# Hybrid decoder layer on one core: the last two token tiles take v's first weight chunks in turn, the convolution's sum of squares is multiplied later, and a quartet's first sum queues behind the split of its first block

## The chip, the cores and the metric

The kernel runs on one core of one Trainium2 chip. The metric is device time in microseconds (us), as the median of several runs; before the change it is 2063.5 us over three runs (2060.89 to 2068.44). Everything is fp32. To keep fp32 precision, TensorE multiplies operands that are split into a rounded high part and the remainder (fp32r hi and lo), and each logical product is three matmuls: hi·hi, hi·lo, lo·hi. Engines are named as in the profile: PE is TensorE (PEld its weight loads), ACT ScalarE, DVE VectorE, POOL GpSimd, SP the sync engine that issues nearly all DMAs.

## The reference

One decoder layer over 512 tokens, model width 2048. Only the first part is touched by the change:

```python
hn = rms_norm(x, norm_mix_pre)                 # (512, 2048)
proj = hn @ w_in                               # 2048 -> 6 x 1024
q, k, v, gate_b, gate_c, hc = split(proj)
a = rms_norm(diff_attention(q, k, v, lam, rel_bias), subln_gain) * (1 - lambda_init)
c = rms_norm(gate_b * short_conv(gate_c * hc, conv_w), conv_norm_gain)
mix = concatenate([a, c]) @ w_out
x = x + rms_norm(mix, norm_mix_post)
f = (silu(rms_norm(x) @ w_gate) * (rms_norm(x) @ w_up)) @ w_down
x = x + rms_norm(f, norm_ffn_post)
```

## The kernel before

**Stages.** The tokens are four tiles t = 0 to 3 of 128. `first_norm(t)` squares a tile on ACT (L225), scales its rows on DVE (L131), transposes it in 16 pieces on PE (L233, banks `pt_pre`), splits the result into hi and lo in `acts` (ACT L100, DVE L101), and copies the transposed tile back into the buffer of `x` (ACT L236). Half of v is multiplied plainly: `v_part(t, q4)` is 12 matmuls of 512 columns (L125 to L127) of tile t with chunk q4 of v's weights. Chunks 0 and 1 lie in the four ring tiles, chunks 2 and 3 in the spots a3, s, a4, a5. `v_out(t)` splits a finished bank `pv` (ACT, then DVE) and stores it. Order before: tiles 0 and 1 complete; then tile 2 is normed and takes its four chunks, then tile 3 is normed and takes its four.

**Quartets.** The rest of the input projection runs as 22 "quartets" q = 0 to 21: 256 columns of `w_in` as a 2 x 2 block problem, done in Strassen's way with seven products instead of eight. The products carry the numbers i = 1, 2, 5, 7, 6, 3, 4; the text writes (q, i). Each is 24 matmuls of 256 columns. `in_order` lists them: (0,1), (1,1), (0,2), (1,2), then (0,5), (0,7), (0,6), (0,3), (0,4), the same five of quartet 1, then whole quartets in the order 1, 5, 7, 2, 6, 3, 4. The names of banks are `pi_a`, `pi_b`, `pi_d`.

A product needs two operands. The weight side `w_i` is made per product by `in_prepare(n)`: a sum or difference of blocks on DVE (`in_combine`: L317 for s1, which (q,5) takes; L319, L321, L323 for the following ones, each on the one before), a hi cast on ACT (L100) and a lo subtraction on DVE (L101). It lies in one of four ring tiles, so at most four are ahead. The token side consists of sums of the halves of the transposed tiles, made once: `i1` (tiles 2, 3 less 0, 1: L249, split L254 apart into `acts`), `i3` (L254 and spots a0, a1), `i2` (L258, spots a2, a3; (q,6) takes it), `i4` (L262, spots a4, a5; (q,4) takes it). `in_gather` takes results out of the banks; L375 copies `pi_a` and so waits for a product's end.

**What sets the order.** The code is traced in the order written; a scheduler in the framework then lays each engine's instructions in one queue, by its own estimates of when they will be ready. After that every engine is strictly first in, first out.

**The convolution.** Quartets 0 to 11 are h, c, b four times. `in_finish` of each b multiplies the gate in (L421), squares on ACT (L423) and adds to `sqacc` on DVE (L429). The last one starts `conv_norm`, a side generator that advances one `yield` per product: it multiplies the four tiles of `sqacc` with a column of ones (L452, bank `p4`, in the profile `p`), takes the root on POOL, puts it on diagonals (DVE L456), multiplies with ones again (L461, bank `prc`) and scales the eight rows of y (DVE L465).

Of the kernel before, what the change touches and what calls it, by code (L numbers as in the profile page):

```python
# [21 lines left out]
NT = S // P  # L22
# [33 lines left out]
def trunk(ctx: ExitStack, tc: tile.TileContext, a, out):  # L56
# [41 lines left out]

    def split(hi, lo, src):
        nc.scalar.copy(hi, src)  # L100
        nc.vector.tensor_tensor(out=lo, in0=src, in1=hi.bitcast(F32), op=ALU.subtract)  # L101

    def rsqrt_mean(ss, n, width, eps, name):
        v = small.tile([P, n], F32, tag=f"v{n}", name=f"v_{name}")
# [115 lines left out]
    def first_norm(t):  # L220
        xn = spot(f"a{2 * (t % 2)}")
        ss = small.tile([P, 2], F32, tag="ss2", name=f"ss_{t}")
        for c in range(2):
            cs = slice(c * 1024, (c + 1) * 1024)
            nc.scalar.activation(xn[:, cs], xts[t][:, cs], AF.Square, accum_out=ss[:, c : c + 1])  # L225
        nc.vector.tensor_add(ss[:, 0:1], ss[:, 0:1], ss[:, 1:2])
        r = rsqrt_mean(ss[:, 0:1], 1, D, EPS, f"pre{t}")
        for k4 in range(4):
            scale_rows(xn, xts[t], r, gB, k4)
            b = aux_bank(f"pt_pre{t}_{k4}")  # L230
            for i in range(4):
                k = 4 * k4 + i
                nc.tensor.transpose(b[:, i * P : (i + 1) * P], xn[:, k * P : (k + 1) * P], ident)  # L233
            sl = slice(4 * k4, 4 * k4 + 4)
            split(*(x_[:, t, sl, :].rearrange("p k n -> p (k n)") for x_ in (ffn_hi, ffn_lo)), b)
            nc.scalar.copy(xts[t][:, k4 * 512 : (k4 + 1) * 512], b)  # L236
# [30 lines left out]
    def bias_rows():  # L267

        t = spot("r0")
        oh, rb, vec = t[:NB, :VL], t[:NB, VL : VL + NH], t[:NH, 1024 : 1024 + VL]  # L270
        nc.sync.dma_start(oh, a["bucket_rows"])
        nc.sync.dma_start(rb, a["rel_bias"])
        for i in range(2):
            b = aux_bank(f"pvec_{i}")
            nc.tensor.matmul(b[:NH, : VL // 2], lhsT=rb, rhs=oh[:, i * (VL // 2) : (i + 1) * (VL // 2)], start=True, stop=True)
            nc.vector.tensor_copy(vec[:, i * (VL // 2) : (i + 1) * (VL // 2)], b[:NH, : VL // 2])
        d1 = dram.tile([NH, VL], F32, name="d1")
        nc.scalar.dma_start(d1, vec)
        d2 = dram.tile([P, NH, VL], F32, name="d2")
        nc.scalar.dma_start(d2, bass.AP(d1.tensor, d1.offset, [[0, P], [VL, NH], [1, VL]]))  # L280
        return d2
# [31 lines left out]
    def in_combine(q, s):  # L313
        (p11, p21), (p12, p22) = ((r[:, :, :P], r[:, :, P:]) for r in in_raws[q])
        if s == 1:
            it["s1"] = in_slot("s1").rearrange("p (k m) -> p k m", k=8)
            nc.vector.tensor_add(it["s1"], p21, p22)  # L317
        elif s == 3:
            nc.vector.tensor_sub(p21, p11, p21)  # L319
        elif s == 2:  # L320
            nc.vector.tensor_sub(p21, p22, p21)  # L321
        else:
            nc.vector.tensor_sub(p12, p12, p21)  # L323

    def in_prepare(n):
        if n >= len(in_order):
            return
        q, i = in_order[n]
        (p11, p21), (p12, p22) = ((r[:, :, :P], r[:, :, P:]) for r in in_raws[q])
        src = {1: p11, 2: p12, 3: p12, 4: p22, 5: it.get("s1"), 6: p21, 7: p21}[i]  # L330
        if i == 7 and q >= 2:
            in_combine(q, 3)
        if i == (3 if q == in_last else 6):
            in_combine(q, 2)
        if i == 3:
            in_combine(q, 4)
        w = ring_tile(16, P, f"w_i{q}_{i}", "still").rearrange("p (a k) m -> p a k m", a=2)
        split(w[:, 0], w[:, 1], src)
        in_ops[n] = w
        if i == 4 and q + 2 <= in_last:  # L340
            load_in(q + 2)
# [103 lines left out]

    def conv_norm():

        yield
        p4 = aux_bank("p4")
        sqacc = it["sqacc"]  # L450
        for t in range(NT):
            nc.tensor.matmul(p4[:, t : t + 1], lhsT=sqacc[:, t * P : (t + 1) * P], rhs=ones[:, 0:1], start=True, stop=True)  # L452
        rc = rsqrt_mean(p4[:, :NT], NT, 1024, EPS, "conv")
        dg = in_slot("sqacc").rearrange("p (t n) -> p t n", n=P)
        for t in range(NT):
            nc.vector.tensor_scalar_mul(dg[:, t, :], ident, rc[:, t : t + 1])  # L456
        yield
        yield
        yield
        prc = aux_bank("prc")  # L460
        nc.tensor.matmul(prc, lhsT=ones, rhs=dg.rearrange("p t n -> p (t n)"), start=True, stop=True)  # L461
        for p in range(4):
            for j in range(2):
                y = it["y", p][:, j, :]
                nc.vector.scalar_tensor_tensor(  # L465
                    out=y, in0=prc, scalar=gcv[:, 2 * p + j : 2 * p + j + 1], in1=y, op0=ALU.mult, op1=ALU.mult
                )
            if p % 2:
                yield
# [10 lines left out]
    def in_proj(_):  # L480
        ready = 4
        for n, (q, i) in enumerate(in_order):
            in_product(n)
            yield
            in_gather(n)
            if n == 2:
                in_combine(0, 1)
                in_combine(0, 3)
            if q == 0 and i in (6, 3):
                in_combine(1, {6: 1, 3: 3}[i])  # L490
            elif 0 < q < in_last and i == 3:
                in_combine(q + 1, 1)
            while ready < n + (3 if n < 4 else 4):
                in_prepare(ready)
                ready += 1
            if n == 3:
                i2(0)
                i2(1)
            if n == 4:
                i4(0)  # L500
                i4(1)
            if i == 5 and q > 0:
                in_finish(q - 1)
            if n == 8:
                small_inputs()
            if q == in_last and i == 2:
                conv_split(0)
            if q == in_last and i == 3:
                conv_split(1)
                preloaded["o0_2"] = load_chunk(*out_spec(0, 2))  # L510
        in_finish(in_last)
# [49 lines left out]
        lambda n: [spot(f"a{ {3: 0, 2: 2, 4: 4}[n] + i}", F32R) for i in range(2)],  # L561
    )

    for t in range(2, NT):
        first_norm(t)
        if t == 2:
            d2 = bias_rows()
            load_in(0)
        else:
            i1(0, (0,))  # L570
            i1(1, (0,))
            i3(0)
            i3(1)
            v_out(0)
            v_out(1)
            v_out(2)
            load_in(1)
        for q4 in range(4):
            v_part(t, q4)
            if t == NT - 1 and q4 < 2:  # L580
                in_prepare(2 * q4)
                in_prepare(2 * q4 + 1)
            if t == NT - 1 and q4 == 1:
                i1(0, (1,))
                i1(1, (1,))
    v_out(3)
    add_job([], in_proj, ahead=0)

# [760 lines left out]
```

## Time and profile before

| what | value |
|---|---|
| median of three runs | 2063.5 us (2060.89 to 2068.44) |
| the profiled execution | 2065.88 us, of which 2063.8 us from first to last instruction |
| mean granted TensorE clock in it | 0.993 |
| ACT busy, DVE busy | 49%, 83% |
| DMA | 346.11 MB, mean 168 GB/s |

In a timeline row stand the start in us, the busy us, engine, line, operation, out<-in, shape and count, and in brackets how long the engine sat idle before it and what ended that. A row of the waits view gives the engine and line that waited, for whom, and then total us, times, longest us. A row of windows gives each engine's busy us in a stretch, then the granted clock (PEclk, 1.00 is full speed), the DMA share and GB/s.

### The profile page before, as it was taken

How to read it: one execution, taken by the hardware profiler on the slowest of the kernel's cores; microseconds unless marked ns; L12 is line 12 of the kernel's file. 1: busy time of each engine (PE TensorE's matmuls, PEld its weight loads, DVE VectorE, ACT ScalarE, POOL GpSimd, SP SyncE). 2: the span in 40 equal slices, each digit the busy share in tenths (PEclk: the TensorE clock that was granted, in tenths of full speed). 3: DMA queues.
4: the chain of work that ended last, by engine and by line, in shares of the span. 5: the costliest groups of instructions: out<-in, count | busy, mean ns of one | idle time of the engine just before them, and what ended most of it. 6: DMA issues, size and time to landing. Idle time of an engine off the chain costs nothing.

```text
span 2063.8 us, 37998 instructions
## 1 busy us (share of the span) xinstructions
PE 2010.3 (97%) x16158; PEld 1941.6 (94%) x16158; DVE 1713.5 (83%) x2141; ACT 1008.1 (49%) x1421; POOL 24.9 (1%) x44
## 2 busy tenths in 40 slices
PE   7999999999999998999999999999999999999998
PEld 5899999999788887999999999999999999999996
DVE  6898889887676689989889989989888687878886
ACT  5555454445576464454455545545545344334442
POOL 0000000000000000000000000000000000000000
PEclk9999999999999999999999999999999999999999
DMA  7533333444663643654554545546546937648354
GB/s 247 156 123 99 107 123 121 166 165 145 207 212 102 233 167 108 186 159 139 174 158 150 170 151 166 175 130 189 164 126 194 346 111 255 210 124 304 108 185 154
DMA packets 310026, 346.11 MB, mean 168 GB/s; under 512 B 12985, under 2 KB 271033, under 8 KB 307425
## 3 DMA queue, kind: packets, MB, share of 16 engines
q1 hardware_dynamic: 308544, 338.95, 50.7%
q10 hardware_dynamic: 1312, 4.74, 0.7%
q8 instruction: 126, 2.06, 0.4%
q14 instruction: 44, 0.35, 0.1%
HBM read 283.87 MB, written 62.41 MB: 168 GB/s over the span
## 4 chain that ended last, share of the span: by engine, by line
PE 74%; DVE 13%; DMA 6%; issue 3%; ACT 2%; SPq 1%; POOL 0%; DVEq 0%; POOLq 0%; ACTq 0%
PE pb L127 6%; PE pb L125 6%; PE pb L126 6%; PE pd L126 6%; PE pd L127 6%; PE pd L125 6%; PE pa L125 5%; PE pa L126 5%; PE pa L127 5%; PE pi_b L127 2%; PE pi_b L126 2%; PE pi_b L125 2%; DVE w L101 2%; DVE w_i L101 2%; PE pi_a L127 2%
## 5 line engine op out<-in xcount | busy, mean ns | idle before, releaser
L100 ACT CAST w<-raw_q 128x1024 fp32r<-128x1024 f32 x130 | 136.7, 1052 | 163.3 <-PE pb L127 72.5
L127 PE MATMUL pb<-acts,w 128*128 128x256 f32 x704 | 195.7, 278 | 3.7 <-DVE w L101 3.7
L125 PE MATMUL pb<-acts,w 128*128 128x256 f32 x704 | 195.4, 278 | 1.6 <-ACT w L100 1.6
L127 PE MATMUL pa<-acts,w 128*128 128x256 f32 x704 | 195.0, 277 | 1.9 <-DVE w L101 1.8
L126 PE MATMUL pb<-acts,w 128*128 128x256 f32 x704 | 195.3, 277 | 0.0
L125 PE MATMUL pa<-acts,w 128*128 128x256 f32 x704 | 194.9, 277 | 0.3 <-ACT w L100 0.3
L127 PE MATMUL pb<-x,w 128*128 128x256 f32 x704 | 194.8, 277 | 0.3 <-DVE w L101 0.2
L125 PE MATMUL pb<-x,w 128*128 128x256 f32 x704 | 194.6, 276 | 0.0
L126 PE MATMUL pb<-x,w 128*128 128x256 f32 x704 | 194.6, 276 | 0.0
L126 PE MATMUL pa<-acts,w 128*128 128x256 f32 x704 | 194.5, 276 | 0.0
L126 PE MATMUL pd<-w_d,acts 128*128 128x256 f32 x640 | 179.1, 280 | 3.4 <-DVE w_d L101 3.4
L125 PE MATMUL pd<-w_d,acts 128*128 128x256 f32 x640 | 178.6, 279 | 1.3 <-DMA acts<-hx 1.3
L127 PE MATMUL pd<-w_d,acts 128*128 128x256 f32 x640 | 178.5, 279 | 0.6 <-DMA acts<-hx 0.6
L101 DVE TENSOR_TENSOR w<-raw_q,w 128x1024 fp32r<-128x1024 f32 x130 | 158.1, 1217 | 4.1 <-ACT w L100 4.0
L127 PEld LDWEIGHTS pb<-acts,w 128*128 128x128 f32 x704 | 133.3, 189 | 4.1 <-DVE w L101 4.1
L125 PEld LDWEIGHTS pb<-acts,w 128*128 128x128 f32 x704 | 133.2, 189 | 1.8 <-ACT w L100 1.8
L127 PEld LDWEIGHTS pa<-acts,w 128*128 128x128 f32 x704 | 132.1, 188 | 2.5 <-DVE w L101 2.5
L126 PE MATMUL pd<-w_d,x 128*128 128x256 f32 x480 | 133.5, 278 | 0.0
L125 PE MATMUL pd<-w_d,x 128*128 128x256 f32 x480 | 133.3, 278 | 0.0
L127 PE MATMUL pd<-w_d,x 128*128 128x256 f32 x480 | 133.2, 278 | 0.0
L126 PEld LDWEIGHTS pb<-acts,w 128*128 128x128 f32 x704 | 133.2, 189 | 0.0
L127 PEld LDWEIGHTS pb<-x,w 128*128 128x128 f32 x704 | 132.4, 188 | 0.6 <-DVE w L101 0.6
(322 smaller groups left out, 6895.5 us busy)
## 6 DMA issues: line engine op xcount, KB each, us to landing
raw_q<-in_w_gate SPq DMA_DIRECT2D x44, 1024.0 KB, 5.5
r_i<-in_w_in SPq DMA_DIRECT2D x22, 1024.0 KB, 5.4
raw_i<-in_w_in SPq DMA_DIRECT2D x22, 1024.0 KB, 5.2
post<-in_w_up SPq DMA_DIRECT2D x22, 1024.0 KB, 5.2
pre<-in_w_up SPq DMA_DIRECT2D x22, 1024.0 KB, 5.9
hx<-spare SPq DMA_DIRECT2D x20, 896.0 KB, 8.4
hx<-m SPq DMA_DIRECT2D x20, 896.0 KB, 9.5
raw_o<-in_w_out SPq DMA_DIRECT2D x16, 1024.0 KB, 5.4
```

Of the source, the lines that this page charges most:

```text
L100: nc.scalar.copy(hi, src)
L101: nc.vector.tensor_tensor(out=lo, in0=src, in1=hi.bitcast(F32), op=ALU.subtract)
L125: nc.tensor.matmul(o, lhsT=lhi, rhs=rhi, start=start, stop=False, **kw)
L126: nc.tensor.matmul(o, lhsT=lhi, rhs=rlo, start=False, stop=False, **kw)
L127: nc.tensor.matmul(o, lhsT=llo, rhs=rhi, start=False, stop=stop, **kw)
```

## The change

Four edits in the first 360 us; the arithmetic is the same.

- **v in turn.** Tile 3 is normed right after the first chunk of tile 2, and its `i1` and `i3` follow. Tiles 2 and 3 then take chunk 0/1, 2 and 3 in turn. `i2`, and the sums s1 and the next difference of quartet 0, are traced before the last chunks, `i4` within the first products; `v_out(2)` comes after tile 2's last chunk. From the third product on (before: the fifth) one operand more is kept ahead.
- **The sum of squares later.** `conv_norm` waits six products instead of one before `p4`, and six instead of three before `prc`.
- **First sums behind a split.** `split` returns its DVE instruction, and s1 of the next quartet (L317) is put behind the last split that was traced, that of (q+1, 1), in DVE's queue. Before, the scheduler was free to put it earlier.

```diff
     def split(hi, lo, src):
         nc.scalar.copy(hi, src)
-        nc.vector.tensor_tensor(out=lo, in0=src, in1=hi.bitcast(F32), op=ALU.subtract)
+        return nc.vector.tensor_tensor(out=lo, in0=src, in1=hi.bitcast(F32), op=ALU.subtract).ins
...
-        split(w[:, 0], w[:, 1], src)
+        it["split"] = split(w[:, 0], w[:, 1], src)
...
     def conv_norm():
-        yield
+        for _ in range(6):
+            yield
         p4 = aux_bank("p4")
...
-        yield
-        yield
-        yield
+        for _ in range(6):
+            yield
         prc = aux_bank("prc")
...
-            if n == 2:
-                in_combine(0, 1)
-                in_combine(0, 3)
             if q == 0 and i in (6, 3):
                 in_combine(1, {6: 1, 3: 3}[i])
             elif 0 < q < in_last and i == 3:
-                in_combine(q + 1, 1)
-            while ready < n + (3 if n < 4 else 4):
+                with tc.issue_after(it["split"]):
+                    in_combine(q + 1, 1)
+            while ready < n + (3 if n < 2 else 4):
                 in_prepare(ready)
                 ready += 1
-            if n == 3:
-                i2(0)
-                i2(1)
-            if n == 4:
-                i4(0)
-                i4(1)
+            if n in (1, 2):
+                i4(n - 1)
...
-    for t in range(2, NT):
-        first_norm(t)
-        if t == 2:
-            d2 = bias_rows()
-            load_in(0)
-        else:
-            i1(0, (0,))
-            i1(1, (0,))
-            i3(0)
-            i3(1)
-            v_out(0)
-            v_out(1)
-            v_out(2)
-            load_in(1)
-        for q4 in range(4):
-            v_part(t, q4)
-            if t == NT - 1 and q4 < 2:
-                in_prepare(2 * q4)
-                in_prepare(2 * q4 + 1)
-            if t == NT - 1 and q4 == 1:
-                i1(0, (1,))
-                i1(1, (1,))
+    first_norm(2)
+    d2 = bias_rows()
+    load_in(0)
+    v_part(2, 0)
+    first_norm(3)
+    for tau in range(2):
+        i1(tau, (0,))
+        i3(tau)
+    v_out(0)
+    v_out(1)
+    load_in(1)
+    v_part(2, 1)
+    for q4 in range(2):
+        v_part(3, q4)
+        in_prepare(2 * q4)
+        in_prepare(2 * q4 + 1)
+    for tau in range(2):
+        i1(tau, (1,))
+    for t in (2, 3):
+        v_part(t, 2)
+    i2(0)
+    i2(1)
+    in_combine(0, 1)
+    in_combine(0, 3)
+    v_part(2, 3)
+    v_out(2)
+    v_part(3, 3)
     v_out(3)
```

What the queues hold now, at three places. First ACT, from the end of v into the first products. In the names, `w_i0_6` is the weight operand of (0,6), `a2` to `a5` are the token sums of `i2` and `i4`, `pi_a0` and `pi_a1` the banks of quartets 0 and 1. Before:

```order
L100 CAST x3_i23_255<-pv_3_107 128x512
L100 CAST w_i0_5_665<-s_i31_662 128x1024
L100 CAST a2_i32_696<-x0_i14_108 128x1024
L100 CAST w_i0_7_692<-raw_i0_0_393 128x1024
L375 COPY s_i31_662<-pi_a0_588 128x256
L375 COPY s_i31_662<-pi_a1_613 128x256
L100 CAST a2_i32_696<-x1_i16_182 128x1024
L100 CAST w_i0_6_730<-raw_i0_0_393 128x1024
```

and after the change:

```order
L100 CAST x2_i22_253<-pv_2_106 128x512
L100 CAST x3_i23_255<-pv_3_107 128x512
L100 CAST a2_i31_553<-x0_i14_108 128x1024
L100 CAST a2_i31_553<-x1_i16_182 128x1024
L100 CAST w_i0_5_678<-s_i33_560 128x1024
L375 COPY s_i33_560<-pi_a0_599 128x256
L100 CAST w_i0_7_681<-raw_i0_0_393 128x1024
L375 COPY s_i33_560<-pi_a1_624 128x256
L100 CAST a4_i34_650<-x0_i14_108 128x1024
L100 CAST w_i0_4_771<-raw_i0_1_394 128x1024
L100 CAST a4_i34_650<-x1_i16_182 128x1024
L100 CAST w_i0_6_712<-raw_i0_0_393 128x1024
```

The token sums of `i4` (a4) and the operand of (0,4) have moved ahead of the operand of (0,6), and the casts of the last two v banks now stand in a row.

DVE holds the partners of these casts. Between the copies above and the operand of (0,6) stood before

```order
L101 TENSOR_TENSOR w_i0_7_692<-raw_i0_0_393,w_i0_7_692 128x1024
L258 TENSOR_TENSOR x1_i16_182<-x3_i23_255,x1_i16_182 128x1024
L321 TENSOR_TENSOR raw_i0_0_393<-raw_i0_1_394,raw_i0_0_393 128x8x128
L262 TENSOR_TENSOR x0_i14_108<-x0_i14_108 128x1024
L101 TENSOR_TENSOR a3_i33_697<-x1_i16_182,a2_i32_696 128x1024
L101 TENSOR_TENSOR w_i0_6_730<-raw_i0_0_393,w_i0_6_730 128x1024
```

and now

```order
L101 TENSOR_TENSOR w_i0_7_681<-raw_i0_0_393,w_i0_7_681 128x1024
L101 TENSOR_TENSOR a5_i35_651<-x0_i14_108,a4_i34_650 128x1024
L262 TENSOR_TENSOR x1_i16_182<-x1_i16_182 128x1024
L321 TENSOR_TENSOR raw_i0_0_393<-raw_i0_1_394,raw_i0_0_393 128x8x128
L101 TENSOR_TENSOR w_i0_4_771<-raw_i0_1_394,w_i0_4_771 128x1024
L101 TENSOR_TENSOR a5_i35_651<-x1_i16_182,a4_i34_650 128x1024
L101 TENSOR_TENSOR w_i0_6_712<-raw_i0_0_393,w_i0_6_712 128x1024
```

so `i4` is finished before the split for (0,6), where before it was finished behind it. Behind these rows DVE goes on with L323, L380, L387, L317 (s1 of quartet 1), the split of (0,3), L383 and the split of (1,5).

Third, PE. Where (0,6) gives over to (0,3), PE had before the 24 matmuls of (0,3) without a break, and (1,5) after (0,4). Now one matmul of (1,5), bank `pi_b1`, stands within (0,3):

```order
L127 MATMUL pi_d0_778<-a2_i31_553,w_i0_6_712 128x256
L125 MATMUL pi_b0_715<-acts_72,w_i0_3_742 128x256
L126 MATMUL pi_b0_715<-acts_72,w_i0_3_742 128x256
L125 MATMUL pi_b1_882<-acts_72,w_i1_5_807 128x256
L127 MATMUL pi_b0_715<-acts_72,w_i0_3_742 128x256
```

And the sum of squares stood between (12,2) and (12,6),

```order
L126 MATMUL pi_a12_3137<-acts_72,w_i12_2_3163 128x256
L127 MATMUL pi_a12_3137<-acts_72,w_i12_2_3163 128x256
L452 MATMUL p4_3253<-ones_78,x3_i23_255 128x1 x4
L125 MATMUL pi_a12_3137<-a2_i32_696,w_i12_6_3192 128x256
L126 MATMUL pi_a12_3137<-a3_i33_697,w_i12_6_3192 128x256
```

and stands now between (13,5) and (13,7), five products on:

```order
L126 MATMUL pi_b13_3376<-acts_72,w_i13_5_3315 128x256
L127 MATMUL pi_b13_3376<-acts_72,w_i13_5_3315 128x256
L453 MATMUL p4_3401<-ones_78,x3_i23_255 128x1 x4
L125 MATMUL pi_b13_3376<-a0_i27_456,w_i13_7_3344 128x256
L126 MATMUL pi_b13_3376<-a1_i28_457,w_i13_7_3344 128x256
```

On DVE the two L429 that finish `sqacc` stand where they stood, behind the split of (12,6); `prc` comes between (14,1) and (14,5), where it was ahead of (13,1), and the eight L465 stand between L323 of quartet 14 and the split of (14,6).

## The prediction

> **What bounds the kernel now.** First the page, for who is busy; then PE's own waits; then the windows and PE's timeline where those waits lie.
>
> ```profile
> PE 2010.3 (97%) x16158; PEld 1941.6 (94%) x16158; DVE 1713.5 (83%) x2141; ACT 1008.1 (49%) x1421; POOL 24.9 (1%) x44
> ```
>
> PE works nearly without a break, so an edit that removes no matmul can only win PE's gaps. The waits of PE over the whole span, longest first:
>
> ```profile
> PE pt_pre L233 <- DVE a_i L131: 9.6, 1, 9.6
> ...
> PE p L452 <- issue: 2.9, 1, 2.9
> PE pi_b L127 <- DVE w_i L101: 2.8, 3, 1.5
> ...
> PE pi_d L127 <- DVE w_i L101: 1.2, 1, 1.2
> ...
> PE pi_b L125 <- ACT w_i L100: 0.3, 1, 0.3
> ```
>
> The 9.6 us at the start are out of the change's reach. The other four rows, 7.2 us, all lie in the input projection, which it reorders. The windows place them and show the clock:
>
> ```profile
> 45.00:50.00 5.00, 5.00 (x27) 3.04 (x26) 3.02 (x6) 3.12 (x6) 0.00 (x0) 1.00 0.04 0
> ...
> 90.00:95.00 5.00, 3.47 (x30) 3.28 (x29) 5.00 (x7) 2.10 (x2) 0.00 (x0) 1.00 0.71 217
> 95.00:100.00 5.00, 4.63 (x38) 4.22 (x36) 5.00 (x9) 1.34 (x2) 0.10 (x1) 1.00 0.41 119
> 100.00:105.00 5.00, 4.21 (x36) 4.21 (x37) 4.57 (x8) 3.11 (x5) 0.00 (x0) 1.00 0.32 113
> 105.00:110.00 5.00, 3.76 (x33) 3.56 (x32) 5.00 (x7) 3.22 (x4) 0.00 (x0) 1.00 0.16 44
> 320.00:325.00 5.00, 3.04 (x14) 3.08 (x15) 3.49 (x6) 1.91 (x3) 0.93 (x1) 0.61 0.74 229
> 325.00:330.00 5.00, 5.00 (x34) 5.00 (x33) 3.10 (x8) 1.32 (x2) 0.09 (x1) 0.71 0.57 194
> ```
>
> From 90 to 110 DVE is full and PE is not: DVE is late with the first quartets' operands. From 320 to 330 there is a second loss beside the wait: the granted clock falls to 0.61 and 0.71.
>
> **The first quartets.** PE's timeline, with the first matmul of (0,5), of (0,3), the four stops, and the first of (1,3):
>
> ```profile
> 83.45 0.28 PE L125 MATMUL pi_b<-acts,w_i 128*128 128x256 f32 x1
> ...
> 91.61 0.28 PE L125 MATMUL pi_b<-acts,w_i 128*128 128x256 f32 x1
> ...
> 93.52 0.39 PE L127 MATMUL pi_b<-acts,w_i 128*128 128x256 f32 x1 [1.53 <-DVE w_i L101]
> ...
> 99.40 0.39 PE L125 MATMUL pi_b<-acts,w_i 128*128 128x256 f32 x1 [0.28 <-ACT w_i L100]
> ...
> 100.79 0.39 PE L127 MATMUL pi_b<-acts,w_i 128*128 128x256 f32 x1 [0.88 <-DVE w_i L101]
> ...
> 107.86 0.39 PE L127 MATMUL pi_d<-a_i,w_i 128*128 128x256 f32 x1 [1.24 <-DVE w_i L101]
> ...
> 110.55 0.28 PE L125 MATMUL pi_b<-acts,w_i 128*128 128x256 f32 x1
> ```
>
> Three products without a wait take 91.61 - 83.45 = 8.16 us: 2.72 us each, 0.113 us a matmul. From (0,5) to (1,3) are eight products, 21.8 us; they took 27.1. So 5.3 us are lost here, 3.9 in waits and the rest in restarts. That is the most this part can win. Why DVE was idle before, and at what pace it works after:
>
> ```profile
> 59.53 1.91 PE L233 MATMUL pt_pre<-ident,a_i 128*128 128x128 f32 x16
> ```
>
> ```profile
> 60.78 1.89 DVE L101 TENSOR_TENSOR acts<-pt_pre,acts 128x512 fp32r<-128x512 f32 x3 [6.25 <-ACT acts L100]
> ...
> 92.25 1.22 DVE L101 TENSOR_TENSOR w_i<-raw_i,w_i 128x1024 fp32r<-128x1024 f32 x1
> 93.39 0.41 DVE L380 TENSOR_TENSOR x_i<-x_i 128x256 f32<-128x256 f32 x1
> 93.73 1.22 DVE L101 TENSOR_TENSOR a_i<-x_i,a_i 128x1024 fp32r<-128x1024 f32 x1
> ```
>
> DVE waited 6.25 us for tile 3's transposes, behind all of tile 2's v. The change puts them after one chunk, three chunks (36 matmuls, about 8 us) earlier, so DVE can start the token sums sooner. PE's work up to (0,5) is the same in number, and I find no new wait there: (0,5) still starts at 83.45. But ACT's queue has changed too:
>
> ```profile
> 83.65 0.37 ACT L375 COPY s_i<-pi_a 128x256 f32<-128x256 f32 x1 [2.34 <-PE pi_a L127]
> 84.42 1.06 ACT L100 CAST a_i<-x_i 128x1024 fp32r<-128x1024 f32 x1 [0.40 <-DVE x_i L258]
> ```
>
> The second L375 waits for the fourth product, in either order. Before, the casts of (0,5) and (0,7) were ahead of it; now the cast of `i4` and all that follows stand behind it, and DVE stands behind ACT. I follow the new queues by these durations (a 1024-wide DVE step takes 1.14 us before the next, a 256-wide one 0.34):
>
> - ACT: L375 to 84.0, cast of `i4` to 85.1. DVE from 85.1: five 1024-wide steps, then the split of (0,6) from 90.8 to 92.0. Its hi cast, behind L321, is done at 89.6.
> - PE: (0,6) is due at 88.9, its third matmul, the first with lo, at 89.1. It stops twice, about 0.7 and 2.2 us, and goes on at 92.0.
> - PE ends (0,6) at 94.5, does two matmuls of (0,3) and comes at 94.7 to the stray one of (1,5). For that DVE does L323, L380, L387, L317 from 91.9 to 95.0 and ACT casts to 96.1: 1.4 us of waiting.
> - From there no operand is late. The closest is (1,6), split done by 105.7, due at 106.9. (1,3) starts at 109.4, and with 0.1 us for each of three restarts at 109.7.
>
> So this part gives 110.55 - 109.7 = 0.8 us, not 5.3: the idle time of DVE before 60 is won, but given back to waits behind ACT. Its ends are -1 (each of the two chains a step of 1.14 us later) and 5.3 (no wait).
>
> On SP the loads of quartet 2 now stand behind all stores of v and four small loads. They need the buffer that the split of (0,6) frees at 92.0 in any case, and their operands are due behind (1,4), after 109; I cost this at nothing, cover some 10 us. Holding one operand more from the third product on uses ring tiles that are free by then, and is in the order above.
>
> **The sum of squares.** The rows around it:
>
> ```profile
> 312.67 0.28 PE L126 MATMUL pi_b<-a_i,w_i 128*128 128x256 f32 x1
> 313.30 0.38 PE L127 MATMUL pi_b<-a_i,w_i 128*128 128x256 f32 x1 [0.35 <-DVE w_i L101]
> ...
> 318.74 0.28 PE L127 MATMUL pi_a<-acts,w_i 128*128 128x256 f32 x1
> 321.95 1.84 PE L452 MATMUL p<-ones,x_i 128*128 128x1 f32 x8 [2.94 <-issue]
> 323.66 0.56 PE L125 MATMUL pi_a<-a_i,w_i 128*128 128x256 f32 x1
> ...
> 328.13 0.28 PE L125 MATMUL pi_a<-a_i,w_i 128*128 128x256 f32 x1
> ...
> 333.93 1.02 PE L461 MATMUL prc<-x_i,ones 128*128 128x512 f32 x2
> ```
>
> ```profile
> 309.62 1.23 DVE L317 TENSOR_TENSOR s_i<-r_i,r_i 128x1024 f32<-128x1024 f32 x1 [3.50 <-DMA r_i<-in_w_in]
> ...
> 312.02 1.22 DVE L101 TENSOR_TENSOR w_i<-raw_i,w_i 128x1024 fp32r<-128x1024 f32 x1
> ...
> 321.17 0.68 DVE L429 TENSOR_TENSOR x_i<-x_i,x_i 128x512 f32<-128x512 f32 x1
> ...
> 336.29 5.35 DVE L465 SCALAR_TENSOR_TENSOR x_i<-prc,gcv,x_i 128x512 f32<-128x512 f32 x8
> ```
>
> "issue" hides DVE: the last L429 ends at 321.85, PE starts at 321.95. After it come the narrow matmuls and 21 normal ones at 0.21 us each. From 318.85 to 328.13 are 9.3 us. Unhindered, the 21 take 2.4, and the eight narrow passes 1.0 if each takes what a transpose does (1.91/16 = 0.12 us at 59.53). So 5.9 us go away if `p4` finds its sum ready. Five products later is 13.6 us, about 332; the sum has 10 us in hand. On DVE, L105 reads `p4` and now stands behind the split of (13,6); the next split behind it is that of (13,3), and PE has three products, 8.2 us, between `p4` and that. So a DVE that waits there holds nobody. If the narrow ones cost their 1.84 us still, it is 5.0.
>
> **First sums behind a split.** At 309.62 L317 of the next quartet held DVE 3.5 us for a transfer; the split behind it came late, and PE lost 313.30 - 312.67 - 0.11 = 0.5 us. With L317 behind the split, that goes. What L317 now waits for, it would have waited for anyway; behind it stand its own quartet's operands, due two products (5.4 us) later.
>
> **The sum.** 0.8 + 5.9 + 0.5 = 7.2 us: 2065.88 - 7.2 = 2058.7 for an execution like the profiled one. That lies 2.4 us above the median of the runs, and its largest loss hangs on when one transfer landed, so in a median run I take some of the 5.9 as absent already: between 2063.5 - 7.2 = 2056.3 and 2058.7, I forecast **2057.5 us**. Half a per cent is 10.3 us, about what a measurement of this kernel can tell from no change.
>
> **The rivals.**
>
> *All waits of the first quartets go* (0.15). For it: DVE's 6.25 idle us exceed the 5.3 lost. Against it: the queue of ACT above. Gain 5.3 + 5.9 + 0.5 = 11.7, so 2065.88 - 11.7 = 2054.2, and down to 2063.5 - 11.7 = 2051.8 as a median.
>
> *The eight scalings meet (14,6)* (0.14). L465 takes 5.35 us on DVE, now right ahead of the split of (14,6), which PE wants three products (8.2 us) and two matmuls after `prc`. Before, L465 began 1.3 us after `prc` ended (336.29 against 334.95); then 1.3 + 5.3 + 1.2 = 7.8 us, a reserve of 0.6. A DVE two steps (2.3 us) later makes PE wait 1.7, and a clock drop like that at 323.66 (21 matmuls at +0.1) adds 2.1: 3.8 us, 2061.3.
>
> *The clock falls at (0,6) and stays low while waits follow* (0.04); this one ends slower. At 321.95 a wait of 2.94 us and the narrow matmuls halved the clock; (0,6) would have 2.9 us. If half speed lasts from there to the end of (1,6), 142 matmuls cost 0.1 us more each, 14.2, less the 1.4 of the next wait that it swallows: 2058.7 + 12.8 = 2071.5. It decides if low clock lasts over 7 us or so. Against it: four stops up to 1.53 us left PEclk at 1.00 from 90 to 110, and matmuls split this one in two. [...] At 321.95 the trace shows the drop after 2.94 us with narrow work behind.
>
> *The clock falls at the transposes* (0.05). Tile 3's 16 transposes now come 12 matmuls after tile 2's and the bias rows:
>
> ```profile
> 45.58 1.47 PE L233 MATMUL pt_pre<-ident,a_i 128*128 128x128 f32 x12
> 46.98 0.70 PE L275 MATMUL pvec<-r_i 32*8 32x320 f32 x2
> ```
>
> If such work counted as idle, about 5 of 7.5 us from 45.6 on would, and a drop would cost as at 323.66, 2.1 us: 2060.8. Against it, 45 to 50 holds over 2 us of it (the two rows) at PEclk 1.00. [...]
>
> That `p4` waits still, in its new place, would need DVE 10 us late (0.02).
>
> **How the numbers follow.** Forecast 0.60, the named rivals 0.40. The range 2051.5 to 2063.5 reaches from the first rival's median to no gain at all. Faster by over 0.5% means under 2053.2: the lower part of the first rival and little else, 0.14. Slower by over 0.5% needs over 2073.8, above even the slow rival: 0.02.
>
> **What would show it.** Right: PE's wait at L453 gone and PEclk 1.00 from 310 to 340; L317 no longer ahead of its split; PE stops at (0,6) for 2 to 3 us and at a `pi_b` L125 for about 1.4; (1,3) starts near 109.7. Wrong: (1,3) before 107 or after 111.7; a wait of PE after 345 behind L465; PEclk under 0.9 anywhere between 45 and 340.

## The result, and the profile after

The changed kernel takes 2054.93 us in the median of six runs (2053.49 to 2057.99); the kernel before, run beside it, 2064.64 us (2059.61 to 2068.44). The ratio is 0.9961, with a 95% interval of 0.9949 to 0.9973: by the ratio some 8 us faster (the two medians lie 9.7 us apart), inside the range that was given and within half a per cent. The profiled execution took 2057.99 us, 7.9 us less than that of before, where the sum was 7.2.

So the total came out. The experiments below show that it came out for a partly wrong reason: of the three edits (the change is announced as four, but it lists three) one does it all, and it is the one that was priced at 0.5 us. First the views in which that can be read. The waits of PE in the projection, after; of the four rows of before, two are left, with other names:

```profile
PE pi_d L127 <- DVE w_i L101: 1.8, 1, 1.8
...
PE pi_d L125 <- ACT w_i L100: 0.6, 1, 0.6
```

The wait at the sum of squares and all waits of `pi_b` are gone. PE's timeline around the two that stay, from the first matmul of (0,5) to that of (1,3):

```profile
83.75 0.28 PE L125 MATMUL pi_b<-acts,w_i 128*128 128x256 f32 x1
...
89.93 0.39 PE L125 MATMUL pi_d<-a_i,w_i 128*128 128x256 f32 x1 [0.58 <-ACT w_i L100]
...
92.26 0.39 PE L127 MATMUL pi_d<-a_i,w_i 128*128 128x256 f32 x1 [1.82 <-DVE w_i L101]
...
93.18 0.41 PE L125 MATMUL pi_d<-a_i,w_i 128*128 128x256 f32 x1
...
96.38 0.38 PE L125 MATMUL pi_b<-acts,w_i 128*128 128x256 f32 x1
...
96.72 0.28 PE L125 MATMUL pi_b<-acts,w_i 128*128 128x256 f32 x1
...
110.19 0.28 PE L125 MATMUL pi_b<-acts,w_i 128*128 128x256 f32 x1
```

The two stops at (0,6) are the forecast ones (0.58 and 1.82 us, where 0.7 and 2.2 were expected). The third, at the stray matmul of (1,5) at 96.72, did not happen. Instead the matmuls from 93.18 on take 0.41 us in place of 0.28. The windows of that place, cut where the clock changes, show why:

```profile
89.77:93.18 3.41, 1.42 (x9) 1.22 (x10) 3.41 (x4) 0.59 (x2) 0.00 (x0) 1.00 0.13 32
93.18:96.59 3.41, 3.41 (x19) 3.41 (x17) 3.10 (x5) 2.10 (x2) 0.00 (x0) 0.50 0.54 178
96.59:100.00 3.41, 3.41 (x31) 3.41 (x31) 3.32 (x8) 0.25 (x1) 0.10 (x1) 1.00 1.06 353
```

For 3.41 us the granted clock is exactly half, behind a window of 3.41 us in which PE was busy for only 1.42. PE came to the stray matmul at 96.72, 2.0 us later than forecast, and by then its operand was there: the cast, forecast to end at 96.1, ended at 96.28. One loss took the place of the other.

Around the sum of squares, its narrow matmuls, and two windows where the clock had been 0.61 and 0.71:

```profile
330.51 0.95 PE L453 MATMUL p<-ones,x_i 128*128 128x1 f32 x8
```

```profile
320.00:325.00 5.00, 5.00 (x47) 5.00 (x46) 4.82 (x7) 2.37 (x3) 0.00 (x0) 1.00 0.34 122
325.00:330.00 5.00, 5.00 (x47) 5.00 (x46) 4.93 (x5) 3.43 (x4) 0.00 (x0) 1.00 0.25 100
```

No stop, full clock, and 0.95 us for the eight narrow passes, which took 1.84 at half clock before. And DVE, which feeds them:

```profile
312.18 1.41 DVE L429 TENSOR_TENSOR x_i<-x_i,x_i 128x512 f32<-128x512 f32 x2
...
319.38 1.22 DVE L317 TENSOR_TENSOR s_i<-r_i,r_i 128x1024 f32<-128x1024 f32 x1
...
350.47 5.35 DVE L465 SCALAR_TENSOR_TENSOR x_i<-prc,gcv,x_i 128x512 f32<-128x512 f32 x8
355.74 1.21 DVE L101 TENSOR_TENSOR w_i<-raw_i,w_i 128x1024 fp32r<-128x1024 f32 x1
```

Here is the row that should give pause. The last L429 ends at 313.6, 8.3 us earlier than before (321.85). But that sum was not moved, only the matmuls that read it. PE starts (12,6), ahead of which `p4` used to stand, at 316.91: `p4` would have found its sum ready in its old place too.

### The profile page after: what moved, and what is told of

It reads as the page before. It is cut to its first block, busy times and chain, and to the rows that moved or that the text cites. A ratio compares the mean times of both kernels' runs of the same rounds, so it can differ in the third digit from the quotient of the medians.

```text
span 2056.2 us, 37995 instructions
## 1 busy us (share of the span) xinstructions
PE 2009.8 (98%) x16158; PEld 1942.2 (94%) x16158; DVE 1714.6 (83%) x2141; ACT 1010.1 (49%) x1421; POOL 26.2 (1%) x44
## 4 chain that ended last, share of the span: by engine, by line
PE 83%; DVE 8%; DMA 3%; issue 2%; ACT 2%; SPq 1%; POOL 0%; DVEq 0%; POOLq 0%; ACTq 0%
PE pb L127 6%; PE pb L126 6%; PE pb L125 6%; PE pd L126 6%; PE pd L127 6%; PE pd L125 6%; PE pa L127 5%; PE pa L126 5%; PE pa L125 5%; PE pi_b L125 4%; PE pi_b L127 4%; PE pi_b L126 4%; PE pi_a L125 3%; PE pi_a L127 3%; PE pi_a L126 3%
## 5 line engine op out<-in xcount | busy, mean ns | idle before, releaser
L127 PEld LDWEIGHTS pb<-acts,w 128*128 128x128 f32 x704 | 132.9, 189 | 3.2 <-DVE w L101 3.2
L127 PEld LDWEIGHTS pa<-acts,w 128*128 128x128 f32 x704 | 132.8, 189 | 2.2 <-DVE w L101 2.2
L125 PEld LDWEIGHTS pb<-acts,w 128*128 128x128 f32 x704 | 132.9, 189 | 1.8 <-ACT w L100 1.8
L125 PEld LDWEIGHTS pa<-acts,w 128*128 128x128 f32 x704 | 132.9, 189 | 0.4 <-ACT w L100 0.4
```

The costliest lines, as they stand in the source:

```text
L125: nc.tensor.matmul(o, lhsT=lhi, rhs=rhi, start=start, stop=False, **kw)
L127: nc.tensor.matmul(o, lhsT=llo, rhs=rhi, start=False, stop=stop, **kw)
```

## The experiments

Three stretches of the projection are compared, read off the starts of products in PE's timeline: A from (0,5) to (1,3), eight products; B from (12,2) to (14,6), fifteen products, with `p4` and `prc` in it; C from (14,6) to (15,1), three products behind the eight scalings.

| kernel | A | B | C | ratio to before (95%) |
|---|---|---|---|---|
| before | 27.10 | 49.15 | 8.17 | 1 |
| changed | 26.44 | 43.20 | 8.17 | 0.9961 (0.9949 to 0.9973) |
| e1: v in turn alone | 26.74 | 49.58 | 8.16 | 0.9999 (0.9988 to 1.0009) |
| e2: sum later alone | 26.96 | 44.22 | 12.35 | 0.9997 (0.9988 to 1.0006) |
| e3: split order alone | 26.28 | 43.09 | 8.16 | 0.9962 (0.9949 to 0.9976) |
| e4: v in turn + split order | 26.32 | 43.10 | 8.16 | 0.9963 (0.9950 to 0.9977) |
| e5: sum later + split order | 26.49 | 43.20 | 8.16 | 0.9965 (0.9952 to 0.9978) |
| e6: changed + four orders | 22.21 | 43.20 | 8.16 | 0.9951 (0.9938 to 0.9963) |
| e8: e3 + four orders | 26.75 | 43.10 | 8.16 | 0.9975 (0.9963 to 0.9987) |
| e10: changed, again | 26.32 | 43.21 | 8.16 | 0.9971 (0.9962 to 0.9981) |
| e11: e6, again | 22.27 | 43.21 | 8.16 | 0.9959 (0.9943 to 0.9975) |

### One edit at a time

e1 is the changed kernel with the other two edits undone:

```diff
     def conv_norm():
-        for _ in range(6):
-            yield
+        yield
         p4 = aux_bank("p4")
...
-        for _ in range(6):
-            yield
+        yield
+        yield
+        yield
         prc = aux_bank("prc")
...
-                with tc.issue_after(it["split"]):
-                    in_combine(q + 1, 1)
+                in_combine(q + 1, 1)
```

> Only v in turn (with i2, i4 and the deeper look-ahead); the sum of squares and the first sums as before. Theory (the parts add up, each in its own place): (0,5) to (1,3) shrinks from 27.1 us to about 26.4 as in the changed kernel, one stop of 0.6 and 1.8 us at (0,6) in place of four; p4 still stops PE for about 2.9 us and half clock follows; L317 still takes 3 us or so waiting for a transfer. 0.4 to 0.8 us faster than before, so about 2064. Rival (a DVE that starts earlier stays ahead): the stop at p4 shrinks below 1.5 us and the clock there stays at 1.00; 5 us faster, about 2059.5.

2061.18 us against 2061.57: no change. A is 0.36 us shorter, B 0.43 us longer. DVE's wait for the transfer ("the hold" from here on) is 3.68 us where it was 3.50, and PE's stop 2.93 us where it was 2.94:

```profile
308.38 1.23 DVE L317 TENSOR_TENSOR s_i<-r_i,r_i 128x1024 f32<-128x1024 f32 x1 [3.68 <-DMA r_i<-in_w_in]
...
319.93 0.68 DVE L429 TENSOR_TENSOR x_i<-x_i,x_i 128x512 f32<-128x512 f32 x1
```

```profile
320.71 1.83 PE L452 MATMUL p<-ones,x_i 128*128 128x1 f32 x8 [2.93 <-issue]
```

The theory holds for where the time is lost (its gain of 0.4 to 0.8 us is too small to be seen in the ratio), and the rival falls: DVE's early start in v does not reach as far as the sum of squares, since L317 waits for a transfer in quartet after quartet, 17 times and 37.5 us in all.

e2 is the kernel before with the six and six `yield`s alone.

> Only the sum of squares later (6 and 6 products). Theory: the stop at p4 and the half clock behind it go, 5.9 us; but with L317 free to stand ahead of its split, DVE comes late behind the eight scalings: (14,6) waits 0.5 to 1.9 us, and perhaps (14,3) and (15,1) too. Gain 4 to 5.4 us, about 2059.5. Rival (the edit needs no help): no wait after 345, gain 5.9, about 2058.7. The first quartets keep their four stops and 27.1 us in both.

2061.28 us against 2061.57: no change either. B shrinks by 4.9 us, as wanted, but C grows by 4.2. DVE and PE behind the new place of the scalings:

```profile
347.85 1.23 DVE L317 TENSOR_TENSOR s_i<-r_i,r_i 128x1024 f32<-128x1024 f32 x1 [2.17 <-DMA r_i<-in_w_in]
...
355.39 5.35 DVE L465 SCALAR_TENSOR_TENSOR x_i<-prc,gcv,x_i 128x512 f32<-128x512 f32 x8
360.66 1.21 DVE L101 TENSOR_TENSOR w_i<-raw_i,w_i 128x1024 fp32r<-128x1024 f32 x1
```

```profile
361.93 0.39 PE L127 MATMUL pi_a<-a_i,w_i 128*128 128x256 f32 x1 [2.16 <-DVE w_i L101]
```

```profile
359.38:362.79 3.41, 1.25 (x11) 1.05 (x10) 3.41 (x6) 1.04 (x1) 0.00 (x0) 1.00 0.00 0
362.80:366.21 3.41, 3.41 (x18) 3.41 (x18) 3.41 (x4) 1.05 (x1) 0.00 (x0) 0.50 0.46 134
```

This is the prediction's rival of the eight scalings, come true in a kernel that lacks the third edit: L317 waits 2.17 us for its transfer, everything behind it is late, (14,6) stops for 2.16 us, and half clock follows. It was priced at 3.8 us; it costs 4.2. My expectation for this run had the waits but not the clock: 4 to 5.4 us of gain, where the projection's last product starts 1.5 us earlier than before (504.58, 506.10) and the time shows none; its interval would still allow 2.5 us. In the changed kernel the same split ends at 355.74 + 1.21 = 356.95, and (14,6) starts at 357.39.

e3 is the kernel before with only this:

```diff
-        nc.vector.tensor_tensor(out=lo, in0=src, in1=hi.bitcast(F32), op=ALU.subtract)
+        return nc.vector.tensor_tensor(out=lo, in0=src, in1=hi.bitcast(F32), op=ALU.subtract).ins
...
-        split(w[:, 0], w[:, 1], src)
+        it["split"] = split(w[:, 0], w[:, 1], src)
...
             elif 0 < q < in_last and i == 3:
-                in_combine(q + 1, 1)
+                with tc.issue_after(it["split"]):
+                    in_combine(q + 1, 1)
```

> Only L317 behind the split of its quartet's first block. Theory: the wait of 0.35 us at (12,7) goes and two delays of 0.2 and 0.45 us around 131 and 260 with it; the stop at p4 and the low clock stay, the first quartets too. 0.5 to 1.3 us faster, about 2063.5. Rival (a later s1 makes the products 5 late): stops at pi_b L125 between 110 and 500, 1 us or more in sum, and no gain.

2053.97 us against 2061.57, the whole gain of the change. Both my theory (0.5 to 1.3 us) and its rival (no gain) were wrong. The stop at `p4` is gone with `p4` in its old place:

```profile
311.23 1.41 DVE L429 TENSOR_TENSOR x_i<-x_i,x_i 128x512 f32<-128x512 f32 x2
...
320.16 1.22 DVE L317 TENSOR_TENSOR s_i<-r_i,r_i 128x1024 f32<-128x1024 f32 x1
```

```profile
315.96 0.95 PE L452 MATMUL p<-ones,x_i 128*128 128x1 f32 x8
```

The two L429 run in a row and end at 312.6, 3.3 us ahead of `p4`. How much this one wait held DVE in the kernel before stands in the waits of DVE:

```profile
DVE s_i L317 <- DMA r_i<-in_w_in: 16.1, 9, 3.5
...
DVE s_i L317 <- DMA raw_i<-in_w_in: 11.0, 8, 3.5
```

Seventeen holds, 27.1 us in all. In the changed kernel and in e3 DVE has no such row: 10 us later in the queue, the transfer has landed. Most of the holds cost PE little, because DVE had time to catch up before an operand was due: from (1,3) to (12,2) PE is 1.36 us faster in e3 than before. The hold at 309.62 was followed by the two L429 and by a PE that waits for them.

The order moves more than the hold. Before, L317 and L319 of the next quartet stood ahead of the sum (2.4 us, from 309.62 to 312.02), and a split stood between the two L429 (1.1 us, at 320.04); in e3 these are behind the sum too. So 3.5 us of waiting and 3.5 us of work left the place ahead of `p4`. Either of them is about as long as what PE lost there, 2.94 us at `p4` and 0.64 at (12,7). That this row's place made the sum late is shown; how much of it was the wait and how much the work, no run separates.

### The edits in pairs

e4 is the changed kernel with the old `yield`s, e5 is e3 with the new ones.

> The changed kernel with the sum of squares put back to one and three products. Theory now (the stop at p4 came from L317 waiting ahead of its split, so the sum's new place wins nothing once L317 is behind): no stop at p4 in its old place, PEclk 1.00 from 310 to 340, and the projection as long as in the changed kernel within 0.3 us; about 8 us under before, ratio 0.996. Rival, as forecast (the place of p4 decides): the stop of about 2.9 us and the half clock are back, 6 us more than the changed kernel.

> The sum of squares later and L317 behind its split, v in the old order. Theory now: the same as the split alone, (0,5) to (1,3) 26.3 us with its three or four stops, no stop after 112, no wait behind the eight scalings; ratio 0.996. Rival: the scalings at their new place still make (14,6) late without the deeper look-ahead, 0.5 us or more after 345.

2053.74 and 2053.72 us against 2062.2. The theory formed after e3 holds in both: B is 43.1 to 43.2 us wherever `p4` stands, and C is 8.16. With L317 behind its split, the sum's new place wins nothing, and v in turn wins nothing that the time or the stretch A shows (26.3 to 26.5 us in e3, e4, e5 and the changed kernel).

### What v in turn could have won

ACT's rows in the changed kernel show what holds it there:

```profile
83.95 0.37 ACT L375 COPY s_i<-pi_a 128x256 f32<-128x256 f32 x1 [1.40 <-PE pi_a L127]
84.22 1.05 ACT L100 CAST a_i<-x_i 128x1024 fp32r<-128x1024 f32 x1
86.67 1.05 ACT L100 CAST w_i<-raw_i 128x1024 fp32r<-128x1024 f32 x1 [1.40 <-PE pi_b L127]
...
88.83 1.05 ACT L100 CAST w_i<-raw_i 128x1024 fp32r<-128x1024 f32 x1
```

L375 at 83.95 was named in the prediction. But there is a second wait of the same kind: the cast at 86.67 is that of (0,4). It writes the ring tile that (0,5) must first give back, and it stands ahead of the cast of (0,6) at 88.83. e9 mends the first alone, in a single execution:

```diff
...
+        it["cast"] = late["cast"]
...
-            nc.scalar.copy(it["q1", q], pq["a"][:, :256])
+            with tc.issue_after(it["cast"]):
+                nc.scalar.copy(it["q1", q], pq["a"][:, :256])
```

> The changed kernel with one more order: L375 behind the last cast traced. This is the row that the prediction named as what holds ACT. Prediction's theory (L375 is what makes (0,6) late): the stops at (0,6) shrink from 2.4 to under 0.5 us. Rival (the cast of (0,4), which waits for a ring tile ahead of the cast of (0,6), is the second half): the two stops shrink only to about 0.5 and 1.3 us, and only together with the casts in order, as in e6_queue_order, do they go.

A is 25.63 us; its one time, 2050.7 us, gives no verdict. The stops of PE in A:

```profile
88.85 0.39 PE L125 MATMUL pi_d<-a_i,w_i 128*128 128x256 f32 x1 [0.32 <-ACT w_i L100]
...
90.48 0.38 PE L127 MATMUL pi_d<-a_i,w_i 128*128 128x256 f32 x1 [1.13 <-DVE w_i L101]
...
94.55 0.39 PE L125 MATMUL pi_b<-acts,w_i 128*128 128x256 f32 x1 [1.06 <-ACT w_i L100]
```

The prediction's single cause falls: with L375 out of the way, stops of 0.32 and 1.13 us stay at (0,6). The clock stays whole behind them: the matmuls there take 0.28 to 0.29 us, where those from 93.18 on took 0.41 in the changed kernel. And the forecast third stop, at the stray matmul of (1,5), appears with 1.06 us.

e6 puts the casts in order too, and PE and quartet 1's sums with them:

```diff
...
-        it["split"] = split(w[:, 0], w[:, 1], src)
+        with ExitStack() as order:
+            if "cast" in it and n < 12:
+                order.enter_context(tc.issue_after(it["cast"]))
+            it["split"] = split(w[:, 0], w[:, 1], src)
+            it["cast"] = late["cast"]
+            it["split", i] = it["split"]
...
+            if "pe" in it and n < 12:
+                order.enter_context(tc.issue_after(it["pe"]))
...
-                in_combine(1, {6: 1, 3: 3}[i])
+                with tc.issue_after(it["split", {6: 3, 3: 4}[i]]):
+                    in_combine(1, {6: 1, 3: 3}[i])
```

> The changed kernel with four more orders, for the first twelve products only: on ACT each operand's cast behind the cast of the product before (so (0,4) no longer goes ahead of (0,6)) and L375 behind the last cast traced; on PE each product behind the one before; on DVE quartet 1's sums behind the splits of (0,3) and (0,4). Theory (the gain of the earlier v was given back in the order of the queues): following the queues, the stops at (0,6) shrink from 2.4 to about 0.3, one of 0.4 us stands at (1,6), no drop of the clock; (0,5) to (1,3) takes 22.6 us in place of 26.4, so (1,3) starts near 106.5; 3.8 us under the changed kernel, ratio to before 0.9943. Rival (DVE has no time left there, whatever the order): (1,3) after 109, gain under 1 us.

A is 22.21 us, where eight products without any stop need 21.8. PE's waits have no row of the projection left. (0,6) begins without a gap, and (1,3) begins 4.7 us earlier than in the changed kernel:

```profile
83.25 0.28 PE L125 MATMUL pi_b<-acts,w_i 128*128 128x256 f32 x1
...
88.69 0.28 PE L125 MATMUL pi_d<-a_i,w_i 128*128 128x256 f32 x1
...
105.46 0.28 PE L125 MATMUL pi_b<-acts,w_i 128*128 128x256 f32 x1
```

e6 adds three orders to that of e9 at once, so that the cast of (0,4) is the second cause is argued from its row at 86.67 and not shown by itself.

The median is 2052.07 us. To set this beside the changed kernel, both ran again on one chip.

> The changed kernel once more, beside the next one on the same chip. The projection takes the same time as in its first profile within 0.3 us, except where the windows of the clock fall otherwise: at (0,6) with the half clock (1,3) near 110.2, and if the two stops there lie in two windows, no half clock but a stop of about 1.3 us at the stray matmul of (1,5). Ratio 0.996.

> The kernel of e6_queue_order once more. Projection 4 to 5 us shorter than in the run beside it; median 2 to 5 us below it, ratio to before 0.993 to 0.995. Rival: what it wins in the projection is lost again behind it (median the same within 1 us).

2054.85 us (12 runs) and 2052.17 us (6 runs). The stretches repeat to 0.15 us, and the gain at the end is 2.7 us of the 4 in stretch A. e11's ratio is 0.9959, short of the 0.993 to 0.995 expected, and the intervals of the two ratios overlap. That e6 beats the changed kernel is seen in the trace, in both pairs of medians and in the runs (of the twelve in e10 one, 2053.62 us, lies below the slowest of e11, 2053.71), but the ratios do not settle it.

e8 gives the same orders to e3, with v in the old order.

> The four orders of e6_queue_order and L317 behind its split, but v in the old order (tile 3 behind all of tile 2) and the sum of squares in its old place. Theory (the orders only spend the time that v in turn gives DVE): DVE still begins the token sums late, the stops at (0,3), (1,5) and (1,6) stay, (0,5) to (1,3) takes 26 to 27 us, ratio 0.996 as with the split alone. Rival (the orders alone do it): 22 to 23 us there, ratio 0.994.

A is 26.75 us: the theory holds. Its ratio, 0.9975, is above the 0.996 expected; the interval overlaps that of e3. Added to the third edit one at a time, neither v in turn nor the orders win anything in A (26.3 us with the third edit alone); together they win 4.

### The clock

e7 takes e6 and makes 14 stops:

```diff
...
+    stops = {14 + 7 * (q - 2): 1 + q % 3 for q in range(3, 21) if q not in (11, 12, 13, 14)}
+
+    def in_stop(n):
+        q1 = it["q1", in_order[n][0]][:, :P]
+        for _ in range(stops[n]):
+            nc.gpsimd.tensor_tensor(out=q1, in0=q1, in1=ones, op=ALU.mult)
+        b = aux_bank(f"stop{n}")
+        it["pe"] = nc.tensor.matmul(b[:, 0:1], lhsT=q1, rhs=ones[:, 0:1], start=True, stop=True).ins
...
+            if n in stops:
+                in_stop(n)
```

> The kernel of e6_queue_order with 14 made stops of PE: after the first product of 14 quartets, PE waits for one, two or three GpSimd passes over L375's result (a product with ones, which changes nothing), then does a narrow matmul. Theory (the clock is set by fixed windows of 3.41 us, and a window in which PE is busy under about half halves the next one): every half-clock stretch is 3.41 us long and begins at a whole multiple of 3.4133 us from the others; stops under 1.6 us never lead to one, those of 2 to 3 us only where most of the stop lies in one window, so some do and some of the same length do not. Rival (a stop's own length decides): all stops above one length are followed by half clock, all below are not, and the stretches begin at a fixed time behind the stop.

For eleven of them the windows of 3.41 us were measured: nine were followed by half clock, two were not (2.58 us of PE in the window at 133.68, 2.35 in that at 468.19). The windows with the stop, and those behind it, for three stops of the first kind and one of the second:

```profile
154.16:157.57 3.41, 1.16 (x9) 0.79 (x7) 2.56 (x3) 1.44 (x3) 2.36 (x2) 1.00 0.00 0
157.57:160.98 3.41, 3.41 (x18) 3.41 (x18) 0.00 (x0) 0.00 (x0) 0.00 (x0) 0.50 0.86 281
178.05:181.46 3.41, 0.95 (x6) 0.75 (x6) 3.41 (x3) 2.55 (x4) 2.73 (x3) 1.00 0.00 0
181.46:184.87 3.41, 2.60 (x12) 2.60 (x13) 3.29 (x5) 0.00 (x0) 0.76 (x1) 0.50 0.48 155
184.87:188.28 3.41, 3.41 (x18) 3.41 (x18) 0.00 (x0) 0.01 (x1) 0.00 (x0) 0.50 0.44 152
...
396.51:399.92 3.41, 1.69 (x12) 1.29 (x12) 3.38 (x4) 2.26 (x3) 1.22 (x1) 1.00 0.39 155
399.92:403.33 3.41, 3.41 (x18) 3.41 (x17) 1.62 (x2) 0.00 (x0) 0.00 (x0) 0.50 0.54 193
...
468.19:471.60 3.41, 2.35 (x18) 1.94 (x18) 3.13 (x3) 1.32 (x2) 0.97 (x1) 1.00 0.00 0
471.60:475.01 3.41, 3.41 (x32) 3.41 (x31) 0.27 (x1) 0.84 (x1) 0.00 (x0) 1.00 0.55 169
```

The half clock begins at 157.57 and at 399.92, 242.35 us apart, 71 times 3.4133; the stretches behind all nine of these stops, from 157.57 to 519.38, lie on that grid. Of the eleven windows, all at full clock, those with 1.69 us of PE or less were followed by half clock, those with 2.35 and 2.58 us were not.

Two points of the expectation failed. Not every stretch of half clock is 3.41 us long: the one at 181.46 takes two windows, and the first of the two, itself at half clock, held only 2.60 us of PE. Before, the half clock at `p4` did the same (2.56 us of PE at 321.11). And stops under 1.6 us did lead to half clock: PE's idle time in the window at 396.51, 1.72 us, is one of 0.92 and one of 0.80 us.

What e7 did not give is two stops of one length with different ends. That part is shown by a stop that stands in every kernel here, 1.8 us at the first matmuls of a block of the down projection. In the kernel before and in e6:

```profile
1651.48 0.39 PE L126 MATMUL pd<-w_d,acts 128*128 128x256 f32 x1 [1.80 <-DVE w_d L101]
```

```profile
1648.89:1652.30 3.41, 1.61 (x14) 1.41 (x14) 2.69 (x4) 0.00 (x0) 0.00 (x0) 1.00 1.02 320
1652.30:1655.71 3.41, 3.41 (x19) 3.41 (x18) 3.41 (x4) 1.78 (x2) 0.00 (x0) 0.50 0.57 193
```

```profile
1639.40 0.39 PE L126 MATMUL pd<-w_d,acts 128*128 128x256 f32 x1 [1.80 <-DVE w_d L101]
```

```profile
1634.96:1638.37 3.41, 2.64 (x23) 2.44 (x21) 0.85 (x2) 1.54 (x2) 0.00 (x0) 1.00 0.92 306
1638.37:1641.78 3.41, 2.38 (x20) 2.38 (x21) 3.41 (x4) 0.32 (x1) 0.00 (x0) 1.00 0.90 300
1641.78:1645.19 3.41, 3.40 (x29) 3.20 (x28) 3.41 (x4) 3.06 (x4) 0.00 (x0) 1.00 0.09 33
```

The same stop, to the hundredth. Before, it lies in one window and costs a half-speed stretch; in e6 the edge of two windows, at 1638.37, falls into it, each keeps over 2.3 us of work, and the clock stays. The rival, that the stop's own length decides, falls.

## Why the prediction was right, and where it was not

**The first quartets** (0.8 us forecast, 27.10 - 26.44 = 0.66 measured). The stops at (0,6) came as worked out from the queues, and (1,3) began at 110.19 where 109.7 was forecast, 0.3 of the difference being a later start of (0,5). Three things under that sum were wrong. The third stop was replaced by half clock, which the text had held unlikely, as a rival with 0.04, because four stops up to 1.53 us had left the clock whole. That argument compared the lengths of stops; in these profiles it was a question of how much of one window they empty: the windows of 3.41 us around those four held at least 2.17 us of PE, the one at (0,6) 1.42. The rival was right that the clock falls and wrong that it stays: it is back after one window, so the slow side of the forecast was not there. A granted clock under 0.9 between 45 and 340 had also been named as a sign that the prediction is wrong, and it is there: 0.82 from 90 to 95, 0.84 from 95 to 100. Next, L375 does not account for the stops at (0,6) alone, as e9 shows. Last, the gain in A cannot be put down to v in turn: alone it wins 0.36 us there (e1), and the third edit without it wins 0.82 (e3). That the 0.8 us came out is in part luck.

The rival of the clock at the transposes falls, by the window of the changed kernel that holds twelve of tile 2's and the bias rows, and by the next, 50 to 55, with tile 3's sixteen, also at 1.00:

```profile
45.00:50.00 5.00, 5.00 (x27) 3.05 (x26) 2.61 (x5) 3.12 (x6) 0.00 (x0) 1.00 0.10 1
```

**The sum of squares** (5.9 us forecast; B shrank by 5.95). The size was read rightly from the 9.3 us between 318.85 and 328.13. The cause was not. This is the step that failed: "So 5.9 us go away if `p4` finds its sum ready. Five products later is 13.6 us." The question that was not asked is why the sum was late at 321.85, and the trace of before answers it, for DVE has no idle time from 309.62 to the last L429: the same 3.50 us of waiting for a transfer that the next part priced, and behind it 3.5 us of work that the third edit also moves behind the sum. (In DVE's queue the two L429 do not stand quite as before: the second was one split further back.)

**First sums behind a split** (0.5 us forecast). The hold was followed for one step, to the late split of (12,7), and its cost taken as that stop. That stop is 0.64 us shorter in the changed kernel; with two smaller ones ahead of it (0.44 and 0.23 us) the stretch from (1,3) to (12,2) is 1.36 us shorter, where 0.5 was forecast. But DVE is full here, and the hold was handed on for over 12 us and past `p4`: after 309.62 its first idle time in the trace ends at 323.83. In e3 the row's place is worth 0.82 us in A, 1.36 from there to (12,2) and 6.06 in B, 8.2 us together, and by the ratio 7.8. The two terms were added as if independent. That did no harm to the sum, because the shared loss was counted once, in the other term; but the text gives the 5.9 us to an edit that wins nothing alone, as e2 shows.

**The eight scalings** were given 0.14 and a reserve of 0.6 us. In the changed kernel the reserve is there (about 0.7) and nothing stops. In e2 it is gone.

**Behind the projection** nothing was forecast. There the profiled executions differ by up to 5.7 us between kernels that are alike from that point on: from the start of the projection's last product to the end it took 1552.1 us in e9 and 1557.8 in the changed kernel. (In the kernel before it took 1557.7, so the two profiles that are compared above are level there.) Part of that is the clock: each window at half speed that lies on work costs up to half of 3.41 us (an estimate; in the changed kernel PE did 18 matmuls in the one at 1646.24 and 31 in the next, at full clock), and behind the stop of 1.80 us there was one before (1652.30) and none in e6. What the rest is was not tried.

## What to carry to other kernels

In the kernel before, DVE waited 3.50 us for a transfer at 309.62 while the split behind it had its cast by 308.41 at the latest, and all behind it ran without idle time to the last L429, which ends at 321.85. So a hold is followed down the queue to the first idle row, and not only to the next consumer; and before an edit is credited with removing a stop, ask what made the operand late, since another edit of the same change may remove it already. Edits that share a cause don't add up: each alone and in pairs tells more than the sum. A stop of PE is to be priced with the clock behind it: by an estimate, half of the 3.41 us of a window, up to 1.7 us more than its length for each window at half clock. The two stops at (0,6), 0.58 and 1.82 us, had work between them and still left 1.42 us of PE in one window, and half clock followed; the one of 1.80 us left 1.61 us in one window before, and half clock followed, and 2.64 and 2.38 us in two in e6, and none did.

## What the runs showed of the hardware

- TensorE's granted clock fell to 0.50 in stretches that keep to a grid of 3.41 us: in each of these executions they begin at multiples of 3.4133 us from one another (before: 17.32, 321.11, 785.32, 1652.30 and 2058.49; changed: 93.18, 758.78, 779.26, 789.50, 1608.70, 1646.24 and 2049.02; e7: the nine above). Of the windows at full clock with a made stop in them, those with 1.69 us of busy PE or less were followed by half clock, those with 2.35 and 2.58 us were not. Other windows show no sharper edge: in the changed kernel 1.80 us left the clock whole (772.43), 1.83 us were followed by half clock (755.37).
- Some windows at half clock were followed by a second one: those with 1.92, 2.56 and 2.57 us of busy PE in the kernel before (17.32, 321.11, 785.32) and that with 2.60 us in e7 (181.46). The six windows of the changed kernel at half clock with 3.37 us or more (93.18 to 1646.24) were not.
- Where the windows fell decided what a stop cost. The stop of 1.80 us lay in one window, with 1.61 us of busy PE, in the profiles of before (1648.89), changed (1642.83) and e3 (1637.58), and each time a stretch followed; in that of e6 the edge of two windows, at 1638.37, fell into it, and none followed. The grid lies otherwise in each execution: counted back in steps of 3.4133 us, its first window begins 0.25 us behind the first instruction in the profile of before, and 1.02 us behind it in that of the changed kernel.
- The eight narrow passes of `p4` took 0.95 us at full clock (changed, e3 and e4) and 1.84 at half (before).
